# Hybrid decoder trunk: projection in groups of four row blocks, gates computed inside the last group, head norms and denominators with tokens on partitions, weights queued two tiles on

## The chip, the cores and the metric

The kernel runs on one core of one Trainium2 chip, in one launch. The metric is the device time of the program in microseconds. Before the change the median of three runs is 2245.18 us (2243.61 to 2250.87).

## The reference, cut to what matters

Two decoder layers over 256 tokens of width 2048, all in float32. Layer 0 mixes tokens with an mLSTM matrix memory, layer 1 with a gated linear recurrence; each mixer and each MLP has a modulated norm ahead of it and a gated residual behind it. The modulations come from a condition vector `c` through four 2048 x 6144 matrices.

```python
for layer in range(DEPTH):
    h, gate = ada_modulate(x, c, ada_w[layer, 0], ada_b[layer, 0])
    y = mlstm_mixer(h, ...) if layer % 2 == 0 else rglru_mixer(h, ...)
    x = x + gate * y
    h, gate = ada_modulate(x, c, ada_w[layer, 1], ada_b[layer, 1])
    x = x + gate * sq_relu_mlp(h, mlp_w1[layer], mlp_w2[layer])
return rms_norm(x) * final_g

# mlstm_mixer: one projection, then two chunks of 128 tokens, 8 heads, one state
q, k, v, o, ig, fg = jnp.split(h @ w_in, [...], axis=-1)
li = ig + b_gate[0]
lf = jax.nn.log_sigmoid(fg + b_gate[1])
#   in a chunk: b = cumsum(lf); m_t = running max; p = exp(d - m_t) * (q k^T)
num = w_inter * (q C) + p v
den = w_inter * (q n) + sum(p)
hh = num / max(|den|, exp(-m_t))
hh = hh * rsqrt(mean(hh * hh) + EPS)             # head norm, over the 256 values of a head
return (hh * norm_g * sigmoid(o)) @ w_out
```

## The kernel before

Activations lie transposed, features on partitions and the 256 tokens along the row; `xT[j]` is row block j of 16. A float32 matrix is multiplied in parts that TensorE takes at full pace: `split` (L167) cuts a weight tile of 128 x 2048, in two halves, into a rounded part `whi`, written by ScalarE (L174), and the rest `wlo`, written by VectorE (L175); `pair` (L179) does so for activations. Two halves of two tiles fit (`SPLIT_BUFS = 4`), so a tile is split when TensorE has done with the tile two before it. `mm3` (L192) makes three products of 256 columns for a block of 128 x 128 weights, `mm2` (L198) the same as one of 512 and one of 256.

Weight tiles come by `load` (L159) on the SyncE queue into a pool `raw` of four buffers. The modulations are done a 128 x 2050 tile at a time (`ada_tile`, L120): one DMA of 1025 KB and one VectorE instruction (L127). There are 192 such conditioning tiles. `fill` (L143) hands them out between weight tiles at a pace, and `need` (L149) when a modulation must be there. They land in `raw` too or, during the projection, in two buffers of their own (`adax`).

A scheduler orders each engine's instructions by program position; `tc.high_priority` moves the splits (200 positions) and the conditioning tiles (50) ahead. Each engine then works through its own row in order, so an instruction that waits holds up all behind it on its engine.

The stages that the change touches:

- **Projection of layer 0** (`group`, L487; products at L511). `GROUPS = (2, 4, 4, 4, 2)` row blocks of `h` are multiplied with 5120 columns of q, k, v and a part of o. A group of four has ten weight tiles, a group of two five. Each tile has 12288 columns to stream in products of 256 (q, k, o) or 512 (v). Between groups the partial sums rest in SBUF: ScalarE brings them back into PSUM (L526) and takes them out again (L537), 20 tiles of 128 x 512 a group. The first weight tile is used in float32, unsplit (`DIRECT`), and four products that compute nothing (`idle`, L540) follow group 0.
- **Gates** (L563 to L626). Ahead of the last group one more block (`gblk`) makes the 16 gate rows. Their log-sigmoid, cumulative sum and running maximum are a chain of small VectorE instructions on 8 x 256 (L583 to L613). `rows` goes to DRAM (L615) and comes back broadcast to all partitions: `mlast` (L617), and `MB` for each head (L634). The last group of two stands behind this in the program.
- **Heads** (`scores`, `state`, `head`, `meansq`, `normed`, L631 to L734). For each of eight heads: scores `sp`, transposed keys `kp`, state `cp`, numerator `num` with features on partitions. The denominator `den` (L675 to L677) and the mean square `hss` (L693, L694) are each computed with a matrix of ones as weights, so that every partition holds the same 256 sums, and `em`, `rs`, `rsu` work on 128 x 256 or 128 x 512 of them. Eight blocks of the rest of o (`ogate`, L703) lie in between where the table `OB` puts them.
- **Out projection** (L754 to L768). The first four output blocks are made together from four tiles `awoa` (the quads), the other twelve a tile `awo` each; `residual` (L332) adds each to `xT[j]`, and for the first eight makes `unnormed` for the MLP. All accumulate in five PSUM buffers (`MM_BUFS`).

Of the kernel before, what the change touches and what calls it, by code (L numbers as in the profile page):

```python
# [60 lines left out]
def trunk_kernel(ctx, tc, xT_d, par_d, ada_d, wqkv_d, wg_d, wo_d, awoa_d, awo_d, bwi_d, bg_d, bwo_d,  # L61
# [245 lines left out]
    def modulated(i, j, r, direct=False):  # L307
# [5 lines left out]
        if not direct:  # L313
            return pair(t, bias=mod[i][:, j:j + 1])
        h = act.tile([P, 2, S], F32, name="hdirect", tag="act")[:, 0, :]
        A.activation(h, t, AF.Identity, bias=mod[i][:, j:j + 1])
        return h, pair(h)
# [149 lines left out]
    def group_h(gi):  # L467
        h32 = []
        for kk in range(GROUPS[gi]):
            k = sum(GROUPS[:gi]) + kk  # L470
            if gi == 0:
                h, p = modulated(0, k, r, True)
                h32.append([h])
            else:
                p = modulated(0, k, r)
            hs.append(p)
        return h32

    raws = []

    def tile_ahead(nt, last):

        while len(raws) <= min(nt + AHEAD, last):
            raws.append(load(wqkv_d[len(raws)]))
        return raws[nt]

    def group(gi, h32):  # L487
# [4 lines left out]
        nt = per * k0 // 4  # L492
        width = DM // gn
        for nb in range(per * gn // 4):
            direct = nt in DIRECT
            gh = h32 if direct else [[p[:, 0, :], p[:, 1, :]] for p in hs[k0:k0 + gn]]
            w = tile_ahead(nt, per * (KC if gi == len(GROUPS) - 1 else KC - GROUPS[-1]) // 4 - 1)
            if not direct:
                w = split(w)
            nt += 1  # L500
# [39 lines left out]
    def idle(n, src):  # L540

        t = aux.tile([P, S], F32, name="idle", tag="aux")
        for _ in range(n):
            PE.matmul(t, lhsT=ones, rhs=src, start=True, stop=True)

    with ExitStack() as actx:
        adas.append(actx.enter_context(tc.tile_pool(name="adax", bufs=ADA_BUFS)))
        for gi in range(len(GROUPS) - 1):
            group(gi, group_h(gi))
            if gi == 0:  # L550
                idle(IDLE, ob[-1][:, 0, :])
        h32 = group_h(len(GROUPS) - 1)
        adas.clear()
# [4 lines left out]
    with ExitStack() as mctx:  # L558
        mp = mctx.enter_context(tc.tile_pool(name="mix0", bufs=1))
        scale = DQK ** -0.5  # L560


# [20 lines left out]
        def log1p(e, s, s2, q):  # L583

            V.tensor_scalar(out=s2, in0=e, scalar1=2.0, scalar2=None, op0=ALU.add)
            V.reciprocal(out=s, in_=s2)
            V.tensor_tensor(out=s, in0=s, in1=e, op=ALU.mult)
            V.tensor_tensor(out=s2, in0=s, in1=s, op=ALU.mult)
            V.tensor_scalar(out=q, in0=s2, scalar1=1.0 / 17, scalar2=None, op0=ALU.mult)
            for k in range(7, 0, -1):  # L590
                V.scalar_tensor_tensor(out=q, in0=q, scalar=1.0 / (2 * k + 1), in1=s2,
                                       op0=ALU.add, op1=ALU.mult)
            V.scalar_tensor_tensor(out=q, in0=q, scalar=1.0, in1=s, op0=ALU.add, op1=ALU.mult)
            return q

# [19 lines left out]
        nc.sync.dma_start(out=rows_d, in_=rows)  # L615
# [1 line left out]
        nc.sync.dma_start(out=mlast, in_=rows_d[:, 0, P - 1].partition_broadcast(P))  # L617
# [343 lines left out]
```

## Time and profile before

| | us |
|---|---|
| median of three runs | 2245.18 |
| the profiled execution | 2244.5 |
| its span, first to last instruction | 2242.8 |
| TensorE busy, weight loads busy | 2181.7, 1960.5 |
| VectorE, ScalarE, GpSimd busy | 1722.3, 1286.1, 90.1 |
| MLP of layer 0 and all behind it, from about 488.4 to the end | 1754.4 |

A row of the page or of a view names line, engine, operation and tiles (out<-in), a count, and a duration. "Idle before" is the time in which that engine had nothing to do ahead of the group, with the instruction that ended it. The windows view gives the busy time of each engine in a stretch, in brackets the number of its instructions, then TensorE's granted clock, the DMA engines' share and GB/s. A busy TensorE is not one at its peak, since products overlap: the number of products in a window tells its pace. A float32 product shows as two records, and some records of products are missing.

### The profile page before, as it was taken

How to read it: one execution, taken by the hardware profiler on the slowest of the kernel's cores; microseconds unless marked ns; L12 is line 12 of the kernel's file. 1: busy time of each engine (PE TensorE's matmuls, PEld its weight loads, DVE VectorE, ACT ScalarE, POOL GpSimd, SP SyncE). 2: the span in 40 equal slices, each digit the busy share in tenths (PEclk: the TensorE clock that was granted, in tenths of full speed). 3: DMA queues.
4: the chain of work that ended last, by engine and by line, in shares of the span. 5: the costliest groups of instructions: out<-in, count | busy, mean ns of one | idle time of the engine just before them, and what ended most of it. 6: DMA issues, size and time to landing. Idle time of an engine off the chain costs nothing.

```text
span 2242.8 us, 34191 instructions
## 1 busy us (share of the span) xinstructions
PE 2181.7 (97%) x13606; PEld 1960.5 (87%) x13606; DVE 1722.3 (77%) x2199; ACT 1286.1 (57%) x1997; POOL 90.1 (4%) x70
## 2 busy tenths in 40 slices
PE   7899899899999999999999999999999999999998
PEld 6798799788888889888889999889888889888887
DVE  6777888988898788888889988998875555555554
ACT  6677777345674335665445877756664334665443
POOL 0000010220000000000110000020000000000110
PEclk9999999899999999999999999999999999999999
DMA  8888887897788999998997665776875555555552
GB/s 345 348 325 319 307 300 255 303 337 270 285 284 319 337 322 332 328 334 319 322 335 276 211 229 208 269 276 238 307 284 203 188 188 188 188 188 188 189 188 93
DMA packets 88671, 601.25 MB, mean 268 GB/s; under 512 B 10424, under 2 KB 14648, under 8 KB 16192
## 3 DMA queue, kind: packets, MB, share of 16 engines
q1 hardware_dynamic: 86400, 598.03, 74.3%
q8 instruction: 106, 1.74, 0.3%
q10 hardware_dynamic: 2112, 1.05, 0.2%
q14 instruction: 53, 0.43, 0.1%
HBM read 596.93 MB, written 2.11 MB: 267 GB/s over the span
## 4 chain that ended last, share of the span: by engine, by line
PE 86%; DVE 7%; ACT 3%; issue 2%; DMA 1%; SPq 0%; DVEq 0%; ACTq 0%
PE mm L200 42%; PE mm L201 22%; PE mm L511 8%; DVE wlo L175 3%; PE mm L196 2%; PE mm L195 2%; PE mm L194 2%; DVE adaraw L127 2%; ACT whi L174 1%; PE mm L218 1%; PE mm L217 1%; PE mm L219 1%; DMA adaraw<-in_ada 1%; PE mm L357 0%; DVE hmod L311 0%
## 5 line engine op out<-in xcount | busy, mean ns | idle before, releaser
L200 PE MATMUL mm<-pair,whi 128*128 128x512 f32 x4272 | 1496.3, 394 | 5.0 <-DVE pair L188 3.2
L201 PE MATMUL mm<-pair,wlo 128*128 128x256 f32 x4272 | 1195.9, 280 | 0.8 <-DVE wlo L175 0.8
L175 DVE TENSOR_TENSOR wlo<-raw,whi 128x1024 fp32r<-128x1024 f32 x736 | 900.2, 1233 | 380.1 <-ACT whi L174 375.9
L174 ACT ACTIVATE whi<-raw 128x1024 fp32r<-128x1024 f32 x736 | 771.9, 1057 | 609.7 <-PE mm L200 476.7
L200 PEld LDWEIGHTS mm<-pair,whi 128*128 128x128 f32 x4272 | 802.6, 188 | 190.7 <-DVE pair L188 4.7
L201 PEld LDWEIGHTS mm<-pair,wlo 128*128 128x128 f32 x4272 | 804.7, 188 | 1.7 <-DVE wlo L175 1.1
L127 DVE SCALAR_TENSOR_TENSOR adaraw<-adaraw,cbc 128x2050 f32<-128x2050 f32 x192 | 439.7, 2291 | 50.7 <-DMA adaraw<-in_ada 41.7
L511 PE MATMUL mm<-pair,whi 128*128 128x256 f32 x736 | 136.0, 288 | 10.7 <-ACT pair L187 5.7
L511 PEld LDWEIGHTS mm<-pair,whi 128*128 128x128 f32 x736 | 115.8, 194 | 12.9 <-ACT pair L187 6.3
L194 PE MATMUL mm<-pair,whi 128*128 128x256 f32 x432 | 123.1, 285 | 0.0
L195 PE MATMUL mm<-pair,whi 128*128 128x256 f32 x432 | 122.0, 282 | 0.0
L196 PE MATMUL mm<-pair,wlo 128*128 128x256 f32 x432 | 121.4, 281 | 0.0
L511 PE MATMUL mm<-pair,wlo 128*128 128x256 f32 x368 | 104.0, 288 | 2.9 <-DVE wlo L175 2.9
L336 DVE SCALAR_TENSOR_TENSOR xall<-mm,mod,xall 128x256 f32<-128x256 f32 x170 | 81.0, 480 | 27.0 <-PE mm L201 18.7
L378 ACT ACTIVATE hsum<-hsum 128x256 f32<-128x256 f32 x121 | 49.2, 413 | 81.7 <-DVE hsum L261 71.3
L291 POOL TENSOR_TENSOR nacc<-nacc,nsq 128x256 f32<-128x256 f32 x52 | 75.6, 1453 | 351.0 <-ACT nsq L282 350.7
L196 PE MATMUL mm<-zhi,wlo 128*128 128x256 f32 x256 | 75.8, 296 | 6.6 <-DVE wlo L175 6.6
L194 PEld LDWEIGHTS mm<-pair,whi 128*128 128x128 f32 x432 | 81.9, 190 | 0.4
L194 PE MATMUL mm<-zhi,whi 128*128 128x256 f32 x256 | 74.9, 297 | 7.6 <-ACT zhi L731 5.5
L195 PEld LDWEIGHTS mm<-pair,whi 128*128 128x128 f32 x432 | 81.8, 189 | 0.0
L196 PEld LDWEIGHTS mm<-pair,wlo 128*128 128x128 f32 x432 | 81.8, 189 | 0.0
L511 PE MATMUL mm<-whi,pair 128*128 128x512 f32 x256 | 81.0, 394 | 0.0
(218 smaller groups left out, 2054.7 us busy)
## 6 DMA issues: line engine op xcount, KB each, us to landing
raw<-in_w SPq DMA_DIRECT2D x220, 1024.0 KB, 5.1
adaraw<-in_ada SPq DMA_DIRECT2D x192, 1025.0 KB, 6.6
raw<-in_wqkv SPq DMA_DIRECT2D x40, 1024.0 KB, 8.5
raw<-in_w1a SPq DMA_DIRECT2D x32, 1024.0 KB, 6.2
raw<-in_bwi SPq DMA_DIRECT2D x28, 1024.0 KB, 5.0
raw<-in_bwo SPq DMA_DIRECT2D x16, 1024.0 KB, 5.1
raw<-in_awo SPq DMA_DIRECT2D x12, 1024.0 KB, 5.5
raw<-in_wo SPq DMA_DIRECT2D x8, 1024.0 KB, 6.2
```

The source lines that it names most:

```text
L127: V.scalar_tensor_tensor(out=raw, in0=raw, scalar=1.0, in1=cbc, op0=ALU.mult, op1=ALU.mult, accum_out=mod[i][:, j:j + 1])
L174: A.activation(hi, sl, AF.Copy)
L175: V.tensor_tensor(out=lo, in0=sl, in1=hi.bitcast(F32), op=ALU.subtract)
L194: PE.matmul(out, lhsT=whi, rhs=hi, start=first, stop=False)
L195: PE.matmul(out, lhsT=whi, rhs=lo, start=False, stop=False)
L196: PE.matmul(out, lhsT=wlo, rhs=hi, start=False, stop=last)
L200: PE.matmul(out, lhsT=whi, rhs=p.rearrange("p a t -> p (a t)"), start=first, stop=False)
L201: PE.matmul(out[:, 0:S], lhsT=wlo, rhs=p[:, 0, :], start=False, stop=last)
L291: G.tensor_tensor(out=self.acc, in0=self.acc, in1=sq, op=ALU.add)
L336: V.scalar_tensor_tensor(out=xT[j], in0=acc[:, a:a + S], scalar=mod[i][:, 32 + j:33 + j], in1=xT[j], op0=ALU.mult, op1=ALU.add)
L378: A.activation(h, h, AF.Relu, bias=c)
L511: PE.matmul(out, lhsT=l, rhs=m, start=clear and kk + n == 0, stop=kk == gn - 1 and n == len(ops) - 1, skip_group_check=True)
```

## The change

- `GROUPS` is (4, 4, 4, 4): eight conditioning tiles now come ahead of the first product. The unsplit first tile and `idle` are gone.
- The gates are a function that is called inside the last group, ahead of its seventh tile (`GATES_AT = 6`); four tiles of the group stand behind it. The table `OB` now starts with 0 and has its eighth block at the last head.
- `den` and the sums of squares are products with one column: the data (`pT`, `qw`, `sq`) are the weights, a column of ones the moving operand. A pair of heads shares a tile `st` of 128 x 8 in PSUM, in one of the five buffers of the accumulators. `em` is made once for all heads, from a transpose of `rows`. The norm is then computed on 128 x 4, and four float32 products with the identity (`br`) spread it over the partitions again.
- All weight tiles from the projection to the first half of the MLP's first layer stand in a list `plan`; `weights` keeps two tiles beyond the present one queued.

```diff
-GROUPS = (2, 4, 4, 4, 2)
-DIRECT = (0,)
+GROUPS = (4, 4, 4, 4)
+GATES_AT = 6
-OB = (1, 1, 0, 1, 0, 1, 0, 1, 0, 1, 0, 1, 0, 1, 0, 0, 0)
+OB = (0, 1, 0, 1, 0, 1, 0, 1, 0, 1, 0, 1, 0, 1, 0, 1, 0)
-QKV_RATE = (1.6, 0.9, 0.9, 0.9, 1)
+QKV_RATE = (0.9, 0.9, 0.9, 0.9)
...
-        if adas and len(done) > 4 or len(done) % 2 < len(adas):
+        if adas and (len(done) > 8 or len(done) % 2 == 0):
...
     def weights(src):
-        return split(load(src))
+        if not plan:
+            return split(load(src))
+        while len(raws) < min(AHEAD + 1, len(plan)):
+            raws.append(load(plan[len(raws)]))
+        plan.pop(0)
+        return split(raws.pop(0))
...
         for nb in range(per * gn // 4):
+            if nb == GATES_AT and between is not None:
+                between()
+            w = weights(wqkv_d[per * k0 // 4 + nb])
...
+    last = 30 + GATES_AT
+    plan += [wqkv_d[n] for n in range(last)] + [wg_d] + [wqkv_d[n] for n in range(last, 40)]
+    plan += [wo_d[j] for j in range(16 - OG)] + [awoa_d[kg] for kg in range(4)]
+    plan += [awo_d[j] for j in range(4, KC)] + [w1a_d[0, j] for j in range(16)]
...
         nc.sync.dma_start(out=rows_d, in_=rows)
-        nc.sync.dma_start(out=mlast, in_=rows_d[:, 0, P - 1].partition_broadcast(P))
+        for c in range(2):
+            nc.sync.dma_start(out=mlast[:, c, :], in_=rows_d[:, c, P - 1].partition_broadcast(P))
+        for c in range(2):
+            gp = aux.tile([P, 2, H], F32, name="gp", tag="aux")
+            PE.transpose(out=gp[:, 0, :], in_=g[:, c * P:(c + 1) * P], identity=ident[0:H, 0:H])
+            PE.transpose(out=gp[:, 1, :], in_=rows[:, 1, c * P:(c + 1) * P], identity=ident[0:H, 0:H])
+            V.tensor_copy(out=gT[:, c, :], in_=gp[:, 0, :])
+            A.activation(em[:, c, :], gp[:, 1, :], AF.Exp, scale=-1.0)
...
+    group(len(GROUPS) - 1, gates)
...
-            PE.matmul(den[:, 0:P], lhsT=ones, rhs=pT[:, 0, :], start=True, stop=True)
-            PE.matmul(den[:, P:S], lhsT=ones, rhs=pT[:, 1, :], start=True, stop=False)
-            PE.matmul(den[:, P:S], lhsT=Cn[:, DV:DV + P], rhs=qw, start=False, stop=True)
-            A.activation(ad, den, AF.Abs)
-            V.scalar_tensor_tensor(out=em, in0=em, scalar=BIG, in1=ad, op0=ALU.min, op1=ALU.max)
-            A.activation(em, em, AF.Square, scale=EPS ** 0.5)
+            PE.matmul(st[:, 1, 0:1], lhsT=pT[:, 0, :], rhs=ones[:, 0:1], start=True, stop=True)
+            PE.matmul(st[:, 1, 1:2], lhsT=pT[:, 1, :], rhs=ones[:, 0:1], start=True, stop=False)
+            PE.matmul(st[:, 1, 1:2], lhsT=qw, rhs=Cn[:, DV:DV + 1], start=False, stop=True)
...
-            PE.matmul(ss, lhsT=ones, rhs=sq[:, 0, :], start=True, stop=False)
-            PE.matmul(ss, lhsT=ones, rhs=sq[:, 1, :], start=False, stop=True)
-            V.scalar_tensor_tensor(out=out, in0=ss, scalar=1.0 / DV, in1=em, op0=ALU.mult, op1=ALU.add)
+            for c in range(2):
+                for eb in range(2):
+                    PE.matmul(st[:, 0, c:c + 1], lhsT=sq[:, eb, c * P:(c + 1) * P], rhs=ones[:, 0:1],
+                              start=eb == 0, stop=eb == 1)
...
-        def normed(h2, rs):
-            rsqrt(rs, rs, 1.0, TINY)
+        def normed(h2, st):
+            A.activation(d, st[:, :, 1, :], AF.Abs)
+            V.scalar_tensor_tensor(out=d, in0=ec, scalar=BIG, in1=d, op0=ALU.min, op1=ALU.max)
+            V.scalar_tensor_tensor(out=d, in0=d, scalar=EPS, in1=d, op0=ALU.mult, op1=ALU.mult)
+            V.scalar_tensor_tensor(out=x, in0=st[:, :, 0, :], scalar=1.0 / DV, in1=d, op0=ALU.mult,
+                                   op1=ALU.add)
+            rsqrt(rs, x, 1.0, TINY)
+            for i in range(2):
+                for c in range(2):
+                    PE.matmul(br[:, i, c * P:(c + 1) * P], lhsT=rs[:, i, c:c + 1].broadcast_to([P, P]),
+                              rhs=ident, start=True, stop=True)
```

How the scheduler's rows change is shown at three places. TensorE, before, first at the scores of head 0 (behind the last group and one o block; L194 to L196 are products of the next o block), then at the numerator of head 0, which 42 more products of that block stand ahead of:

```order
L639 MATMUL sp<-qk_187,qk_191 128x128 x2
L641 MATMUL kp<-ident,qk_191 128x128
L194 MATMUL mm<-pair,whi 128x256
L195 MATMUL mm<-pair,whi 128x256
L196 MATMUL mm<-pair,wlo 128x256
```

```order
L195 MATMUL mm<-pair,whi 128x256
L196 MATMUL mm<-pair,wlo 128x256
L671 MATMUL num<-E,v_195 128x128
L672 MATMUL num<-E,v_196 128x128
L673 MATMUL num<-qw,Cn 128x128
```

TensorE, after, at the same place; its first row is the end of the first o block, which follows the last group:

```order
L204 MATMUL mm<-pair,wlo 128x256
L596 MATMUL gp<-ident,g 128x8 x2
L621 MATMUL sp<-qk_187,qk_191 128x128 x2
L597 MATMUL gp<-ident,rows 128x8
L623 MATMUL kp<-ident,qk_191 128x128
L597 MATMUL gp<-ident,rows 128x8
L641 MATMUL cp<-v_195,kw 128x256
L642 MATMUL cp<-ones,kw 128x1
L652 MATMUL num<-E,v_195 128x128
L653 MATMUL num<-E,v_196 128x128
L654 MATMUL num<-qw,Cn 128x128
```

The o block that stood between the scores and the numerator now stands behind the numerator. In rows behind the block of gates TensorE had five weight tiles and two o blocks up to the numerator, and has four tiles and one o block now.

VectorE, before, at the end of the gate chain (`ls2`, `lf`, `g`, `rows` are the chain; `wlo` belongs to the tile `raw` named beside it, here of the last group; `adaraw` are conditioning tiles):

```order
L591 SCALAR_TENSOR_TENSOR ls2_2346<-ls2_2346 8x256
L127 SCALAR_TENSOR_TENSOR adaraw_2583,mod0_127<-adaraw_2583,cbc_98 128x2050
L593 SCALAR_TENSOR_TENSOR ls2_2346<-ls2_2346,lse_2343 8x256
L127 SCALAR_TENSOR_TENSOR adaraw_2630,mod0_127<-adaraw_2630,cbc_98 128x2050
L599 SCALAR_TENSOR_TENSOR lf_2361<-ls2_2346,li_2340 8x256
L175 TENSOR_TENSOR wlo_2634<-raw_2537,whi_2633 128x1024
L607 SCALAR_TENSOR_TENSOR lf_2361<-ones_85,lf_2361 8x128
L175 TENSOR_TENSOR wlo_2638<-raw_2537,whi_2637 128x1024
L609 TENSOR_TENSOR g_2363<-li_2340,lf_2361 8x128
```

VectorE, after, at the same place (`raw_2614` and `raw_2715` are the second and third o block):

```order
L183 TENSOR_TENSOR wlo_2824<-raw_2614,whi_2823 128x1024
L545 SCALAR_TENSOR_TENSOR ls2_2419<-ls2_2419 8x256
L183 TENSOR_TENSOR wlo_2828<-raw_2614,whi_2827 128x1024
L547 SCALAR_TENSOR_TENSOR ls2_2419<-ls2_2419,lse_2416 8x256
L126 SCALAR_TENSOR_TENSOR adaraw_2678,mod0_127<-adaraw_2678,cbc_98 128x2050
L575 SCALAR_TENSOR_TENSOR lf_2434<-ls2_2419,li_2413 8x256
L612 TENSOR_SCALAR halfg_2685<-par_78 128x16
L583 SCALAR_TENSOR_TENSOR lf_2434<-ones_85,lf_2434 8x128 x2
L585 TENSOR_TENSOR g_2436<-li_2413,lf_2434 8x128 x2
L587 SCALAR_TENSOR_TENSOR rows_2437<-g_2436 8x128
L183 TENSOR_TENSOR wlo_2958<-raw_2715,whi_2957 128x1024
L589 TENSOR_TENSOR rows_2437<-lf_2434,rows_2437 8x128
```

From the gate block's evacuation to the last row of the chain there were four tiles to split and four conditioning tiles; now there are six and four, and the sixth is that of the third o block.

VectorE, before, at the last two heads (`rs`, `em`, `rsu` on 128 x 256 and 128 x 512; all `adaraw` are conditioning tiles):

```order
L695 SCALAR_TENSOR_TENSOR rs_3516<-hss_3655,em_3623 128x256
L175 TENSOR_TENSOR wlo_3969<-raw_3966,whi_3968 128x1024
L175 TENSOR_TENSOR wlo_3973<-raw_3966,whi_3972 128x1024
L271 SCALAR_TENSOR_TENSOR rsu_3660<-rs_3516,rsy_3659 128x512
L127 SCALAR_TENSOR_TENSOR adaraw_4028,mod1_128<-adaraw_4028,cbc_98 128x2050
L272 SCALAR_TENSOR_TENSOR rsu_3660<-rsu_3660,rsy_3659 128x512
L127 SCALAR_TENSOR_TENSOR adaraw_4036,mod1_128<-adaraw_4036,cbc_98 128x2050
L273 SCALAR_TENSOR_TENSOR rs_3516<-rsu_3660,rsy_3659 128x512
```

VectorE, after, at the end of the quads, behind that norm (`mm_3651` and the two behind it are accumulators of the quads, `raw_3771` and `raw_3829` the first two `awo` tiles):

```order
L126 SCALAR_TENSOR_TENSOR adaraw_3908,mod1_128<-adaraw_3908,cbc_98 128x2050
L183 TENSOR_TENSOR wlo_4016<-raw_3829,whi_4015 128x1024
L126 SCALAR_TENSOR_TENSOR adaraw_3920,mod1_128<-adaraw_3920,cbc_98 128x2050
L183 TENSOR_TENSOR wlo_4020<-raw_3829,whi_4019 128x1024
L126 SCALAR_TENSOR_TENSOR adaraw_3927,mod1_128<-adaraw_3927,cbc_98 128x2050
L126 SCALAR_TENSOR_TENSOR adaraw_3935,mod1_128<-adaraw_3935,cbc_98 128x2050
L340 SCALAR_TENSOR_TENSOR xall_80<-mm_3651,mod0_127,xall_80 128x256
L340 SCALAR_TENSOR_TENSOR xall_80<-mm_3652,mod0_127,xall_80 128x256
```

In the changed kernel no conditioning tile stands between the last head's numerator and its norm any more; five stand behind it and ahead of the first residual.

More of the change, by code (lines that the diff above doesn't have):

```diff
@@ L312, in modulated @@
                                op0=ALU.mult, op1=ALU.mult)
[L313 to L317, printed above, removed]
+        return pair(t, bias=mod[i][:, j:j + 1])
     def unnormed(i, j):
@@ L465, in trunk_kernel, with group @@
     ob = [act.tile([P, 2, S], F32, name="th", tag="act") for s in range(OG // 2)]
[L467 to L487, printed above, removed]
+    def group(gi, between=None):
         gn, k0 = GROUPS[gi], sum(GROUPS[:gi])
         per = (4096 + OG * P) // 512
-        nt = per * k0 // 4
         width = DM // gn
+        hs.extend(modulated(0, k0 + kk, r) for kk in range(gn))
+        gh = [[p[:, 0, :], p[:, 1, :]] for p in hs[k0:]]
         for nb in range(per * gn // 4):
[L495 to L500, printed above, removed]
+            if nb == GATES_AT and between is not None:
+                between()
+            w = weights(wqkv_d[per * k0 // 4 + nb])
             def part(kk, o, n):
-                if direct:
-                    return [w[:, kk * width + o:kk * width + o + n]]
                 o += kk % (gn // 2) * width
@@ L538, in group @@
             fill(1, QKV_RATE[gi])
[L540 to L553, printed above, removed]
+    last = 30 + GATES_AT
+    plan += [wqkv_d[n] for n in range(last)] + [wg_d] + [wqkv_d[n] for n in range(last, 40)]
+    plan += [wo_d[j] for j in range(16 - OG)] + [awoa_d[kg] for kg in range(4)]
+    plan += [awo_d[j] for j in range(4, KC)] + [w1a_d[0, j] for j in range(16)]
+    actx = ExitStack()
+    adas.append(actx.enter_context(tc.tile_pool(name="adax", bufs=ADA_BUFS)))
+    for gi in range(len(GROUPS) - 1):
+        group(gi)
     qT = [qk[h // 2][:, h % 2, :] for h in range(H)]
@@ L556, in trunk_kernel, with log1p, gates @@
     vh = [[vs[h // 2 * 2 + t][:, h % 2, :] for t in range(2)] for h in range(H)]
-    with ExitStack() as mctx:
-        mp = mctx.enter_context(tc.tile_pool(name="mix0", bufs=1))
-        scale = DQK ** -0.5
+    rows_d = dram.tile([H, 2, S], F32, name="rows_d")
+    mlast = const.tile([P, 2, H], F32, name="mlast")
+    gT = const.tile([P, 2, H], F32, name="gT")
+    em = const.tile([P, 2, H], F32, name="em")
+    wk = const.tile([P, H], F32, name="wk")
+    def log1p(e, s, s2, q):
+        V.tensor_scalar(out=s2, in0=e, scalar1=2.0, scalar2=None, op0=ALU.add)
+        V.reciprocal(out=s, in_=s2)
+        V.tensor_tensor(out=s, in0=s, in1=e, op=ALU.mult)
+        V.tensor_tensor(out=s2, in0=s, in1=s, op=ALU.mult)
+        V.tensor_scalar(out=q, in0=s2, scalar1=1.0 / 17, scalar2=None, op0=ALU.mult)
+        for k in range(7, 0, -1):
+            V.scalar_tensor_tensor(out=q, in0=q, scalar=1.0 / (2 * k + 1), in1=s2,
+                                   op0=ALU.add, op1=ALU.mult)
+        V.scalar_tensor_tensor(out=q, in0=q, scalar=1.0, in1=s, op0=ALU.add, op1=ALU.mult)
+        return q
+    def gates():
         gblk = block([wg_d], hs)
@@ L581, in trunk_kernel @@
         A.activation(e, e, AF.Exp, scale=-1.0)
[L583 to L594, printed above, removed]
         at = log1p(e, row("ls"), row("ls2"), row("lq"))
@@ L631, in scores @@
         def scores(h):
-            MB = mp.tile([P, 2, S], F32, name="MB", bufs=MB_BUFS)
-            nc.sync.dma_start(out=MB.rearrange("p r t -> p (r t)"),
-                              in_=rows_d[h].rearrange("r t -> (r t)").partition_broadcast(P))
+            MB = mp.tile([P, S], F32, name="MB", bufs=MB_BUFS)
+            nc.sync.dma_start(out=MB, in_=rows_d[h, 0].partition_broadcast(P))
             sp = aux.tile([P, 2, P], F32, name="sp", tag="aux")
@@ L740, in trunk_kernel @@
             if h % 2 == 0:
-                rs = act.tile([P, 2, S], F32, name="rs", tag="act")
-            kw, E, qw, em = sc
+                st = ps.tile([P, 2, 2, 2], F32, name="st", tag="mm")
+            kw, E, qw = sc
             Cn = state(h, kw)
             ogate(OB[1 + 2 * h])
-            hbh, sq, em = head(h, E, qw, em, Cn)
+            hbh, sq = head(h, E, qw, Cn, st[:, h % 2])
             hbs.append(hbh)
```

56 lines of the change are left out of this document (26 added, 30 removed).

## The prediction

> **What bounds the kernel now.** I read the page first, then the windows, the chain, and the timelines around the gates and the heads.
>
> ```profile
> PE 2181.7 (97%) x13606; PEld 1960.5 (87%) x13606; DVE 1722.3 (77%) x2199; ACT 1286.1 (57%) x1997; POOL 90.1 (4%) x70
> ```
>
> TensorE is busy for all but 61 us. What an edit can win is work that it no longer does, and those gaps. The windows show where they lie (time, TensorE, weight loads, VectorE, ScalarE, GpSimd, clock, DMA):
>
> ```profile
> 60.00:70.00 10.00, 3.78 (x26) 3.02 (x24) 8.36 (x10) 2.91 (x4) 0.00 (x0) 0.96 0.93 361
> 70.00:80.00 10.00, 9.96 (x61) 9.95 (x62) 3.95 (x4) 5.42 (x8) 0.00 (x0) 0.69 0.98 412
> 80.00:90.00 10.00, 10.00 (x88) 10.00 (x87) 9.92 (x11) 8.68 (x14) 0.00 (x0) 1.00 0.77 290
> 182.00:244.30 62.30, 58.65 (x385) 52.16 (x384) 47.63 (x44) 40.32 (x60) 0.00 (x0) 1.00 0.82 310
> 260.00:270.00 10.00, 5.85 (x38) 5.85 (x38) 9.84 (x12) 8.55 (x14) 0.00 (x0) 0.83 0.78 275
> 390.00:400.00 10.00, 4.40 (x35) 4.07 (x34) 10.00 (x13) 3.98 (x4) 0.00 (x0) 1.00 0.99 357
> 400.00:410.00 10.00, 6.91 (x30) 6.61 (x31) 7.36 (x10) 2.33 (x4) 0.00 (x0) 0.52 0.92 327
> 430.00:440.00 10.00, 5.94 (x33) 5.74 (x32) 10.00 (x12) 4.29 (x7) 3.87 (x2) 0.73 0.87 307
> 650.00:700.00 50.00, 50.00 (x288) 43.74 (x287) 46.45 (x65) 30.09 (x51) 0.00 (x0) 1.00 0.86 311
> ```
>
> Full pace is 88 products of 256 columns in 10 us, 0.1136 us each. So a projection tile (12288 columns) or an o block (48 such products) is worth 5.45 us. The gate block is 16 pairs of `mm2`; the last row has 288 such products in 50 us, so a pair is 0.347 us and the block 5.6. Behind 510 us I find no gap that the change touches. In 390 to 400 and 430 to 440 VectorE is full while TensorE starves. After each pause the clock falls: 70 to 80 holds 61 products, 3 us short. I charge 3 us for a long pause.
>
> **The start.** The chain:
>
> ```profile
> 5.03 14.80 DMA adaraw<-in_ada
> 19.85 2.30 DVE adaraw L127 x2
> 24.59 31.48 PE mm L511 x176
> 70.03 109.93 PE mm L511 x714
> ```
>
> Now eight conditioning tiles come ahead of the first product, not four. The row of 19.85 is the fourth. Four more are 4.2 MB, 10 us at the 412 GB/s above, so the eighth lands at 29.6 instead of 19.8. Then follow its VectorE instruction (2.3), the pairs and the first split (0.5, 1.05, 1.2): products flow at 36, with half of a cold start still charged at 38.5. Five tiles at 5.45 end at 65.8. Before, five tiles ended and the sixth began at 70.0, cold, in effect 73. **-7.2.** The pause at 56 to 70, when group 1 waited for conditioning, goes: eight are handed out over ten tiles.
>
> A boundary between groups falls at the tenth tile, with an evacuation (0.6), a pair (0.5) and a split (1.06 and 1.23) one behind the other, estimated at +3. At the end of the stage ScalarE's row puts a split behind the evacuation of the tile's first half; that cost some 0.8 us a tile in ten tiles (182 to 244, 62.3 us against 54.5), and will in nine: -1. That group's window stands among the rows above. The gate block took 244.3 to 253.7 for 5.6 us of products; inside a group I charge it 2 us of loss, not 3.8: -1.8. Together **-7.0**. The 40 evacuations and reloads saved (0.6 us each) are on ScalarE beside full TensorE and count nothing but this. The gate block ends at 252 (T below), with one tile more behind it than before, where T was 253.7.
>
> **The gates.** What follows T before, from four timelines:
>
> ```profile
> 253.76 0.38 ACT L260 ACTIVATE gacc<-mm 128x256 f32<-128x256 f32 x1 [2.78 <-PE mm L201]
> 262.25 0.41 ACT L581 ACTIVATE lse<-lse 8x256 f32<-8x256 f32 x1
> 284.63 0.28 DVE L613 TENSOR_TENSOR rows<-lf,rows 8x128 f32<-8x128 f32 x1
> 284.93 0.35 SPq L615 DMA_DIRECT2D rows_d<-rows  x1
> 286.42 1.22 SPq L617 DMA_DIRECT2D mlast<-rows_d  x1
> 287.68 1.10 SPq L634 DMA_DIRECT2D MB<-rows_d  x2
> 295.09 0.70 ACT L646 ACTIVATE E<-MB,gT 128x128 f32<-128x128 f32 x2 [0.54 <-DMA MB<-rows_d]
> 305.33 0.38 PE L671 MATMUL num<-E,v 128*128 128x128 f32 x2
> ```
>
> The chain takes 31.2 us to `rows`, 10.2 more through DRAM to the first exponential, 3 to the numerator: 44. TensorE had 5 tiles and 2 blocks, 38.2 us, to cover it, and reached the numerator at T+51.6, 13.4 lost, most of it elsewhere (260 to 270). Now it has 4 tiles and 1 block, 27.3. The durations:
>
> ```profile
> L175 DVE TENSOR_TENSOR wlo<-raw,whi 128x1024 fp32r<-128x1024 f32 x736 | 900.2, 1233 | 380.1 <-ACT whi L174 375.9
> L174 ACT ACTIVATE whi<-raw 128x1024 fp32r<-128x1024 f32 x736 | 771.9, 1057 | 609.7 <-PE mm L200 476.7
> L127 DVE SCALAR_TENSOR_TENSOR adaraw<-adaraw,cbc 128x2050 f32<-128x2050 f32 x192 | 439.7, 2291 | 50.7 <-DMA adaraw<-in_ada 41.7
> L591 DVE SCALAR_TENSOR_TENSOR ls<-ls 8x256 f32<-8x256 f32 x7 | 2.9, 411 | 0.2
> L586 DVE RECIPROCAL lse<-ls 8x256 f32<-8x256 f32 x1 | 1.7, 1741 | 0.0
> ```
>
> On VectorE stand ahead of `rows`: six tiles to split (14.8), four conditioning tiles (9.2 and 0.3 of read-out) and 10.6 of chain, 35 us. (The same count for before, with four tiles, gives 30 against the 31.2 seen.) It also waits: `lse` is on ScalarE behind two evacuations and two splits, ready at T+12 and not T+8.9, and each split waits for TensorE, the last, of the third o block, for the end of the first at T+29. I get `rows` at T+41. On SyncE a conditioning tile and two `mlast` (1.22 each) stand ahead of `MB`: the exponential at T+52, the numerator at T+55.5, 3 more for the cold clock. TensorE stands from T+30 with nothing else in its row. Lost 58.5 - 27.3 = 31.2 instead of 13.4: **+17.8.** I bound it by 8 (nothing but what TensorE lacks: two of 5.45, less 3) and 26 (each of four conditioning tiles 2 us late).
>
> **The heads.** Rows of a float32 product of 128 columns, of the mean square, and VectorE's in 290 to 410:
>
> ```profile
> 305.55 0.39 PE L672 MATMUL num<-E,v 128*128 128x128 f32 x2
> 305.77 0.39 PE L673 MATMUL num<-qw,Cn 128*128 128x128 f32 x2
> ...
> 361.00 0.68 PE L693 MATMUL hss<-hsq,ones 128*128 128x256 f32 x2
> 361.52 0.59 PE L694 MATMUL hss<-hsq,ones 128*128 128x256 f32 x2
> ```
> ```profile
> L681 DVE SCALAR_TENSOR_TENSOR em<-em,ad 128x256 f32<-128x256 f32 x8 | 3.4, 420 | 0.3 <-ACT ad L680 0.3
> L695 DVE SCALAR_TENSOR_TENSOR rs<-hss,em 128x256 f32<-128x256 f32 x8 | 3.3, 418 | 0.6 <-PE hss L694 0.6
> L271 DVE SCALAR_TENSOR_TENSOR rsu<-rs,rsy 128x512 f32<-128x512 f32 x4 | 2.8, 694 | 2.0 <-ACT rsy L270 1.9
> ```
>
> A head had four products of 0.22 (`den`, `cp` by ones) and 0.9 of `hss`: 1.8 us. Now it has eight of one column. No row shows one; it lies between nothing and the 0.23 of two passes that each keep the 0.1136 pace with their weight load. I take 0.15: 1.2 a head, 8 x 0.6 = 4.8 won, four `br` of 4 x 0.22 lost (3.5), and some 1 for `num`'s shorter partners: **-2.3**, between -10 and +4.
>
> The Trainium skill, TensorE: Matmul & The Clock Gate, section LDWEIGHTS, has a weight load cost by its columns, 128 / 1.2 = 107 ns. By that rule two passes with nothing to stream under are 0.21 us, as dear as the products replaced; the estimate would be 4 us more, 2248. No row here shows an uncovered load.
>
> VectorE is relieved of 8 x 0.84 and four times 2.1, less 24 tiny ones of some 0.15: 11 us. A head now asks 7.9 us of it and 9.2 of TensorE, where both asked 9.5.
>
> **Norm of the last heads and out projection.** The two stretches up to 488.4, and two rows of VectorE:
>
> ```profile
> 305.30:388.00 82.70, 82.70 (x659) 80.17 (x658) 71.18 (x97) 61.28 (x118) 7.79 (x6) 1.00 0.74 265
> 388.00:488.40 100.40, 84.86 (x643) 83.53 (x643) 91.56 (x103) 40.12 (x65) 25.53 (x14) 0.90 0.90 325
> ...
> 398.63 0.69 DVE L273 SCALAR_TENSOR_TENSOR rs<-rsu,rsy 128x512 f32<-128x512 f32 x1
> 411.68 1.66 DVE L336 SCALAR_TENSOR_TENSOR xall<-mm,mod,xall 128x256 f32<-128x256 f32 x4 [0.37 <-PE mm L196]
> ```
>
> From numerator 0 to the MLP before: 183.1 us for 6 blocks (32.7), heads (32) and 768 products (87.2), so 31 lost. 12.6 of it is 390 to 410: conditioning tiles between the pieces of the last norm. That goes: the new order has none there, and an o block and 106 products cover the chain. But the tiles only move. Five of them now stand ahead of the first residual, and the second `awo` block needs the accumulator that this residual frees. From the last `br`, TensorE ends the quads and one block at 22.9; VectorE, splitting and conditioning, comes to the residual at 27.9: 5.4 lost. Then two conditioning tiles a block (4.6), a split (2.4), residual and `unnormed` (1.1) ask 8 us of VectorE against 5.45: 2 to 3 lost in each of four blocks. With 2 for GpSimd's adds I get 17.4 lost there and 5 in the heads, 22.4 against 31: **-8.7**, between -16 and -2. Queueing two on costs nothing by itself: the buffers of `raw` are still four.
>
> **Sum** against the profiled execution, 2244.5, which is 0.7 under the median: -7.0 + 17.8 - 2.3 - 8.7 = -0.2, so 2244. The MLP would begin at 488.2 and runs as before.
>
> **Rivals.** No change is what I forecast, and 0.3% (6.7 us) is about what a measurement can tell. (1) Faster: VectorE, relieved, keeps up in the out projection, whose loss falls to 8, and `rows` comes at T+36 by the plain count of 35: 2244 - 9 - 5 = 2230. For it: its 95% busy rows end at the heads. Against: eight us a block. (2) Slower: the gate chain becomes the bound. Each us of `rows` behind T+41 is one of TensorE; from T+48 the kernel is slower by 6.7. Four conditioning tiles each landing 3 us late would do: 2244 + 12 = 2256. For it: SyncE waits mostly for these two buffers. Against: 41.7 us of 439 is all that VectorE ever waited for them, mostly at the start. (3) One-column products as dear as 0.23: 2248. (4) The start pays nothing, for group 0 waits on DMA: +7, 2251.
>
> **How the numbers follow.** Forecast 0.34, (1) 0.32, (2) 0.20, (3) 0.08, (4) 0.06. Same is the forecast with (3): 0.42; faster is (1): 0.32; slower is (2) with (4): 0.26. The half widths of the terms' bounds, 5 for the start (rival 4 pays it nothing), 9, 7 and 7, add as independent ones to 14; the range goes a little past that and past (1) and (2) on both sides, 2227 to 2261.
>
> **What would show it.** First projection product near 34 to 36; no pause at 56 to 70; TensorE empty for some 20 us or more ahead of numerator 0, released by `E` or `Cn` and behind that `MB`; the last norm without a pause; a wait for the first residuals. Wrong if that first pause is under 10 us (then faster), or if the out projection still holds TensorE for 25 us.

## The result

The changed kernel takes 2270.95 us (median of 4 runs, 2266.32 to 2276.74), the kernel before 2245.6: a ratio of 1.011, 95% interval 1.008 to 1.0141. It is slower by some 25 us, where the forecast was no change (2244) and the range ended at 2261. The profiled execution is the slowest of the four, 2276.74 us with a span of 2275.0, so a comparison of the two traces holds about 6 us more than the medians do.

Four points of the program cut both traces into pieces: T, the evacuation of the gate block; numerator 0; the first product of the MLP of layer 0; the end. Each row is read from the timelines and the span of that kernel's trace.

| | first split product | T | numerator 0 | MLP begins | from there to the end |
|---|---|---|---|---|---|
| before | 33.2 | 253.8 | 305.3 | 488.1 | 1754.8 |
| after | 37.9 | 258.7 | 309.8 | 505.6 | 1769.4 |

Since one tile more lies ahead of T now and one o block more behind numerator 0 (5.45 us each), the pieces compare like this. Up to T: 5.0 - 5.45 = **-0.5**. From T to numerator 0, 51.1 us for 27.3 of work, so 23.8 lost and not 13.4, and 6.6 lost to a low clock behind it: **+17.0**. From there to the MLP 195.8 - 5.45 - 6.6 = 183.7 against 182.7: **+1.0**. From the MLP to the end **+14.6**. Together 32.1 of the spans' 32.2.

### The profile page after: what moved, and what is told of

The parts are those of the page before. It is cut to its first block, busy times and chain, and to the rows that moved or that the text cites. A ratio compares the mean times of both kernels' runs of the same rounds, so it can differ in the third digit from the quotient of the medians.

```text
span 2275.0 us, 34314 instructions
## 1 busy us (share of the span) xinstructions
PE 2191.3 (96%) x13680; PEld 1970.3 (87%) x13680; DVE 1712.6 (75%) x2197; ACT 1258.8 (55%) x1939; POOL 75.3 (3%) x70
## 4 chain that ended last, share of the span: by engine, by line
PE 84%; DVE 8%; ACT 3%; issue 2%; DMA 2%; SPq 0%; DVEq 0%; ACTq 0%
PE mm L208 42%; PE mm L209 21%; PE mm L491 9%; DVE wlo L183 3%; PE mm L204 2%; PE mm L202 2%; PE mm L203 2%; DVE adaraw L126 2%; ACT whi L182 1%; DMA adaraw<-in_ada 1%; PE mm L227 1%; PE mm L226 1%; PE mm L225 1%; DVE hmod L319 1%; DVE pair L196 0%
## 5 line engine op out<-in xcount | busy, mean ns | idle before, releaser
L491 PE MATMUL mm<-pair,whi 128*128 128x256 f32 x768 | 139.6, 285 | 24.9 <-ACT whi L182 22.4
L202 PE MATMUL mm<-pair,whi 128*128 128x256 f32 x432 | 123.4, 286 | 0.0
L203 PE MATMUL mm<-pair,whi 128*128 128x256 f32 x432 | 123.2, 285 | 0.0
L340 DVE SCALAR_TENSOR_TENSOR xall<-mm,mod,xall 128x256 f32<-128x256 f32 x170 | 81.1, 480 | 26.6 <-PE mm L209 19.0
L225 PE MATMUL mm<-unnormed,whi 128*128 128x258 f32 x272 | 77.6, 285 | 0.0
```

The source lines that it names most:

```text
L202: PE.matmul(out, lhsT=whi, rhs=hi, start=first, stop=False)
L203: PE.matmul(out, lhsT=whi, rhs=lo, start=False, stop=False)
L225: PE.matmul(out[:, 0:UX], lhsT=whi, rhs=u[:, 0:UX], start=first, stop=False)
L340: V.scalar_tensor_tensor(out=xT[j], in0=acc[:, a:a + S], scalar=mod[i][:, 32 + j:33 + j], in1=xT[j], op0=ALU.mult, op1=ALU.add)
L491: PE.matmul(out, lhsT=l, rhs=m, start=clear and kk + n == 0, stop=kk == gn - 1 and n == len(ops) - 1, skip_group_check=True)
```

## The profile after

The timelines of the changed kernel around the gates (start, duration, engine, line, instruction; in brackets the idle time ahead of it and what ended it):

```profile
258.73 0.39 ACT L268 ACTIVATE gacc<-mm 128x256 f32<-128x256 f32 x1 [1.57 <-PE mm L209]
287.77 0.28 PE L204 MATMUL mm<-pair,wlo 128*128 128x256 f32 x1
293.55 0.47 PE L596 MATMUL gp<-ident,g 8*128 8x8 f32 x2 [5.49 <-DVE g L585]
296.91 0.28 DVE L589 TENSOR_TENSOR rows<-lf,rows 8x128 f32<-8x128 f32 x1
299.81 3.55 SPq L617 DMA_DIRECT2D MB<-rows_d  x2
305.76 0.69 ACT L628 ACTIVATE E<-MB,gT 128x128 f32<-128x128 f32 x2 [6.07 <-DMA MB<-rows_d]
308.52 1.22 PE L641 MATMUL cp<-v,kw 128*128 128x256 f32 x2 [10.64 <-ACT kw L625]
309.82 0.78 PE L652 MATMUL num<-E,v 128*128 128x128 f32 x2
```

TensorE ends the first o block at 287.8, T+29, as forecast; `rows` is done at T+38.5 (forecast T+41), the exponential stands at T+47 (T+52), the numerator at T+51 (T+55.5). Between 287.8 and 309.8 TensorE has only the scores, transposes and the state of head 0. The windows show that pause, the clock behind it, and two stretches of the MLP (time, TensorE, weight loads, VectorE, ScalarE, GpSimd, clock, DMA share, GB/s):

```profile
290.00:300.00 10.00, 2.57 (x9) 1.82 (x9) 9.48 (x18) 0.36 (x2) 0.00 (x0) 0.50 0.24 86
300.00:310.00 10.00, 1.48 (x5) 1.30 (x6) 3.30 (x6) 2.33 (x9) 0.81 (x2) 0.50 0.87 238
310.00:320.00 10.00, 10.00 (x46) 9.82 (x47) 3.63 (x5) 3.14 (x9) 2.33 (x1) 0.50 0.76 236
320.00:330.00 10.00, 10.00 (x72) 10.00 (x71) 3.37 (x4) 4.52 (x9) 0.00 (x0) 0.79 0.29 98
...
505.60:530.60 25.00, 19.59 (x126) 17.85 (x125) 23.33 (x37) 11.66 (x19) 0.00 (x0) 0.86 0.83 292
605.60:630.60 25.00, 22.07 (x116) 18.70 (x115) 21.66 (x35) 13.47 (x27) 0.00 (x0) 0.93 0.70 261
```

From 310 to 330 there are 118 products where full pace has 176: 58 x 0.1136 = 6.6 us, at a clock of 0.50 to 0.79.

Behind 505 VectorE's own row shows what the MLP waited for:

```profile
505.23 2.36 DVE L183 TENSOR_TENSOR wlo<-raw,whi 128x1024 fp32r<-128x1024 f32 x2 [1.50 <-ACT whi L182]
507.50 2.29 DVE L126 SCALAR_TENSOR_TENSOR adaraw<-adaraw,cbc 128x2050 f32<-128x2050 f32 x1
509.72 0.48 DVE L340 SCALAR_TENSOR_TENSOR xall<-mm,mod,xall 128x256 f32<-128x256 f32 x1
511.69 2.36 DVE L183 TENSOR_TENSOR wlo<-raw,whi 128x1024 fp32r<-128x1024 f32 x2 [1.50 <-ACT whi L182]
513.97 2.29 DVE L126 SCALAR_TENSOR_TENSOR adaraw<-adaraw,cbc 128x2050 f32<-128x2050 f32 x1
516.18 0.42 DVE L279 SCALAR_TENSOR_TENSOR rsu<-ss,rsy 128x256 f32<-128x256 f32 x1
523.96 0.79 PE L208 MATMUL mm<-pair,whi 128*128 128x512 f32 x1 [5.42 <-DVE pair L196]
```

The last residual of the out projection (L340) stands behind a weight tile's split and a conditioning tile, and the norm (L279) behind another of each: it comes 10.6 us after the MLP's first product. TensorE then waits 5.4 us for the first pairs. The two stretches of 25 us in the windows hold 126 and 116 products.

## The experiments

Fifteen kernels ran. Times are medians, ratios against the kernel before on the same chip. The changed kernel's own interval, 1.008 to 1.0141, is 7 us either way, so a gain of a few us against it is not shown by the medians alone.

**e1, the gates earlier.** `-GATES_AT = 6`, `+GATES_AT = 0`.

> The gates are called ahead of the first tile of the last group, not ahead of its seventh; nothing else is changed. In the changed kernel TensorE stood from 287.8 to 309.5 between the first o block and numerator 0, and its clock was 0.50 to 0.79 from 310 to 330, some 6 us more. Theory A (the gate chain lacks cover): ten tiles and a block, 60 us, now cover a chain of about 50, the pause goes and with it the cold clock: 18 to 28 us less, 2243 to 2253. Rival B (VectorE's total of splits, conditioning tiles and chain is the limit, wherever the chain stands): the pause comes back as waits inside the last group, gain under 8 us, 2263 or more.

2259.24 us, ratio 1.0066 (1.0051 to 1.0081): 11.7 won, between the two theories. The gate chain was done at 260.5, long before the o block ended, and yet numerator 0 stood at 296.3, behind two waits of 2.6 and 4.9 us. Two rows of SyncE's timeline in this kernel, and one of its waits from 278 to 292:

```profile
260.50 0.35 SPq L590 DMA_DIRECT2D rows_d<-rows  x1
289.61 0.80 SPq L617 DMA_DIRECT2D MB<-rows_d  x2
```
```profile
SPq L617 <- DVE halfg L612: 5.4, 1, 5.4
```

The broadcasts `MB` waited for `halfg`, the first tile of the heads' own pool, which VectorE wrote right behind the last conditioning tile from `adax`. So the heads could not begin before the group's conditioning tiles were through. That the pool takes the place of `adax` in memory is argued from the code, not tried. Theory A holds for the chain and falls for the pause.

**e2, two o blocks ahead of numerator 0.** Only the table `OB` is that of before.

> Only the table of the o blocks is that of before: two blocks ahead of numerator 0, none at the last head. Theory A: one block more covers the gate chain, the pause ahead of numerator 0 falls by 5.5, and the last norm loses its block, which costs up to 5: 2265 to 2271. Rival B: the block's split on VectorE pushes the chain back as far as it covers, no gain at numerator 0, and the last norm's loss stands alone: 2271 to 2277.

2267.56, ratio 1.0103 (1.0088 to 1.0118): 3.4 won, as by A, but within the changed kernel's interval. Numerator 0 stands at T+50.9 with one block more in the cover.

**e3, no list behind the projection.**

```diff
-    plan += [wo_d[j] for j in range(16 - OG)] + [awoa_d[kg] for kg in range(4)]
-    plan += [awo_d[j] for j in range(4, KC)] + [w1a_d[0, j] for j in range(16)]
```

> The list of weights queued two ahead holds only the projection and the gate block; the o blocks, the out projection and the MLP load a tile where it is split. From the MLP's first product to the end the changed kernel took some 9 to 15 us longer than before, and the out projection waited 3 us at each of four blocks for the split. Theory C (tiles queued two ahead hold the raw buffers that conditioning tiles need, and shift these in VectorE's row to where TensorE waits): 8 to 15 us less, 2256 to 2263, the gates' pause unchanged. Rival D (these waits come from the number of conditioning tiles due there, not from the queue): 2268 to 2274.

2255.06, ratio 1.0045 (1.0028 to 1.0062): 15.9 won, as by C or a little more. Numerator 0 to MLP takes 186.7 us, not 195.8, and MLP to end 1757.0, not 1769.4. The gates' pause is as it was (T+51.5).

**e4, the old groups.** `GROUPS = (2, 4, 4, 4, 2)`, their rates, gates ahead of the last group.

> Groups of 2, 4, 4, 4, 2 with before's rates of conditioning tiles, gates ahead of the last group of two; the unsplit first tile and the idle products stay out, all else as in the changed kernel. Theory E (groups of four pay nothing at the start; the later first product costs what the pause at 56 to 70 cost): the gate block ends within 3 us of where it would by the changed kernel less one tile, 253.3. Five tiles and one block cover the chain, one tile more than in the changed kernel: 2262 to 2269. Rival F (groups of four won the 7 us of the forecast and lost them elsewhere): the gate block ends at 258 or later.

2259.49, ratio 1.0069 (1.0054 to 1.0084). The gate block ends at 250.9, 2.4 us earlier than theory E's 253.3: groups of four pay nothing. (In the ten kernels whose program is that of the changed kernel up to there, T lies between 256.3 and 258.7, so 2.4 is no more than scatter.) Numerator 0 at T+48.3.

**e5 and e6**, e1 and e4 each without the list.

> Gates ahead of the last group (as in e1) and the list ending with the projection (as in e3). Theory: the cover of the gate chain and the queue of weights are two separate costs, 11.7 and 15.9 us, and add up: 2243. Rival: both draw on one thing, VectorE's and the queue's backlog around the heads, so that either edit alone already wins most of it: 2250 to 2255. In e1 the broadcasts MB stood in SyncE's queue from 263 to 289.6 behind tiles queued ahead; if that was all that was left of the pause there, this kernel comes below the sum, 2236 to 2240.

> Groups of before (as in e4), gates ahead of the last group of two, and the list ending with the projection. By the sum of e4 (-11.5) and e3 (-15.9): 2243 to 2245. If groups of four pay for themselves once their gate chain is covered, e5 is faster than this by 5 or more; if they pay nothing, the two agree within 3.

2250.94, ratio 1.0024 (1.0010 to 1.0037), and 2251.66, ratio 1.0033 (1.0021 to 1.0045). They agree within 1 us: the groups pay nothing. Both are 8 us above the sums. That would mean that most of what an earlier gate chain wins and half of what the list costs is paid in one place; but each sum carries the 7 us of the changed kernel, so this is not shown.

**e7, the old head norms**, on e3: `den` and `hss` by a matrix of ones, `em` and `rs` on wide tiles, no `st`.

> As e3 (2255), with denominators and mean squares as before: products with a matrix of ones as weights, sums on all partitions, the norm on 128 x 512. From the traces a head takes about 0.9 us less in the changed kernel, and no norm arithmetic on wide tiles is left on VectorE: if that is so this kernel is 5 to 8 us slower than e3, 2260 to 2263. By my forecast's term, 2.3 us: 2257. Rival (the price of one-column products is that of the products replaced): 2254 to 2256.

2240.63, ratio 0.9977 (0.9967 to 0.9987): not 5 to 8 slower than e3 but 14.4 faster. Every reading of mine on the heads missed. The rows of TensorE showed why: between the transposes of the gates and numerator 0 the scheduler had put 86 products of o blocks, where it puts none in e3 and in the changed kernel. Numerator 0 itself came no earlier, T+49.6. What differed for these products was `st`, which lies among the five accumulators (tag `mm`). That is tried in e9 and e10.

**e8, one tile ahead** behind the projection, not two.

> The list stays, but behind the projection only one tile beyond the present one is queued, not two. Theory C (a tile that waits in one of four raw buffers keeps a conditioning tile out, and these then come late and together): one buffer less is held, half or more of the 16 us comes back, 2256 to 2264. Rival (the order in SyncE's queue alone, whatever is held): 2268 to 2273.

2272.0, ratio 1.0125 (1.0110 to 1.0141). Nothing comes back, so theory C falls: holding one tile instead of two costs the same. No kernel has a list that holds no buffer.

**e9 and e10, `st` moved**, in the changed kernel and in e3.

```diff
-                st = ps.tile([P, 2, 2, 2], F32, name="st", tag="mm")
+                st = aux.tile([P, 2, 2, 2], F32, name="st", tag="aux")
```

> The changed kernel with one edit: st, the tile of a pair's sums, is taken from the three buffers of scores, states and numerators and not from the five of the accumulators. In the built order 96 products of o blocks then stand between the transposes of the gates and numerator 0, where the changed kernel has none. Theory G (st's place among the accumulators keeps the next o block behind numerator 0, and the pause there and the cold clock behind it are the loss): 96 products are 10.9 us that move into a pause of 20, and the clock stays up: 12 to 17 us less, 2254 to 2259. Rival H (the new head norms are slow in themselves: short products, their waits): 2268 to 2272.

> The same edit on e3 (2255). Theory G: as e7, whose old head norms used no accumulator: 2238 to 2243. If the new head norms win the 2.3 us of the forecast by themselves, 1 to 3 below e7's 2240.6. Rival H: 2252 to 2256.

2256.41, ratio 1.0045 (1.0031 to 1.0059), and 2241.92, ratio 0.9981 (0.9971 to 0.9991): 14.5 and 13.1 us won by moving one tile, as by theory G. The windows of e9 at the place of the pause:

```profile
290.00:300.00 10.00, 9.79 (x78) 9.11 (x77) 9.94 (x20) 2.64 (x5) 0.00 (x0) 1.00 0.28 85
300.00:310.00 10.00, 8.47 (x72) 8.22 (x71) 3.92 (x7) 2.88 (x10) 0.82 (x2) 1.00 0.92 244
310.00:320.00 10.00, 9.86 (x80) 9.27 (x80) 6.34 (x9) 8.48 (x20) 1.81 (x2) 1.00 0.88 309
320.00:330.00 10.00, 10.00 (x87) 9.95 (x86) 9.58 (x16) 6.02 (x8) 0.91 (x1) 1.00 0.94 349
```

TensorE holds 150 products in the 20 us where it held 14, and the clock stays at 1.00. Numerator 0 stands at T+50.3 as ever. e10 is faster than both kernels, and e7 agrees with it: with that mended, the new head norms and the old cost the same. Two tenths of a per cent is all that these kernels win on the kernel before.

**e11 and e12**, on e10: the gates ahead of the fifth tile (`GATES_AT = 4`); the rows' way through DRAM on GpSimd's queue.

> As e10, with the gates ahead of the fifth tile of the last group (six tiles behind them, not four). If the gate chain still leaves a pause in e10, two tiles more, 10.9 us, cover it; the order has 48 products there instead of 90, so the net cover is 6 us more: 2233 to 2239. If the pause is gone already or is SyncE's and not VectorE's, no change: within 3 of e10.

> As e10, with the rows' way through DRAM (to rows_d, mlast, MB) on GpSimd's queue, not SyncE's, where it stood behind tiles that waited for buffers. If that wait is part of the pause ahead of numerator 0: 2 to 6 us below e10. If VectorE's rows come too late anyway: within 2 of e10.

2254.94, ratio 1.0043 (1.0029 to 1.0057), and 2249.89, ratio 1.0016 (1.0007 to 1.0025). Both missed, on the slow side. In e12 the trip itself was longer: `rows_d` left at 296.65, `mlast` only at 301.15, and the numerator stood at T+55.4, 5 later. In e11 the numerator stood at T+51.5 and its clock fell to 0.50 behind it; but 196.1 us from there to the MLP, against e10's 173.4, is 15 more than I can account for by products. That stays open.

**e13 and e14, the list without the MLP's tiles**, in the changed kernel and in e9. `- + [w1a_d[0, j] for j in range(16)]`.

> The changed kernel with the list ending at the out projection: only the 16 tiles of the MLP's first half of the first layer leave it. With st mended, the kernel with the list (e9) and the one without (e10) differ by 14.4 us, and the traces put nearly all of it behind the MLP's first product: 1772 us from there to the end with the list, 1758 without, with 22 and 37 products fewer in two stretches of 25 us. Theory J (the list costs through the MLP's tiles: split as soon as they are there, ahead of the norm's own chain on VectorE): 9 to 14 us less, 2257 to 2262. Rival K (it costs in the heads and the out projection, where e3 won 9 of its 16): 2265 to 2271.

> Both edits on the changed kernel: st among the buffers of scores and numerators (e9, 2256.4), and the list without the MLP's tiles. Theory J: 2242 to 2246, as e10. Rival K: 2250 to 2256.

2261.79, ratio 1.0083 (1.0070 to 1.0096): 9.2 won, in the range of J. 2252.87, ratio 1.0036 (1.0024 to 1.0048): 3.5 won, in the range of K. Both intervals meet those of the kernels they are compared with, so the medians do not decide between J and K. In the traces the MLP's part is alike, 1759.1 us to the end (10.3 less) and 1761.0 (11.2 less). But that overstates the gain, since the cut itself moves. TensorE's row in e13, from the last product of the out projection to the first of the MLP:

```profile
497.15 0.28 PE L204 MATMUL mm<-zhi,wlo 128*128 128x256 f32 x1
498.25 0.70 PE L309 MATMUL ss<-nacc,ones 128*128 128x256 f32 x2 [0.81 <-POOL nacc L299]
...
500.95 0.39 PE L225 MATMUL mm<-unnormed,whi 128*128 128x258 f32 x1 [1.57 <-ACT whi L182]
```

TensorE now waits ahead of the MLP's first product, which starts 3.8 us behind the last one of the out projection, in e14 too; in the changed kernel, e9 and e10 it is 0.1. Counted from that last product to the end, e13 and e14 win 6.7 and 7.6 us, not 10.3 and 11.2. And from numerator 0 up to it e14 takes 175.4, e9 175.9 and e10 173.3. The windows of e13, to compare with the two stretches above:

```profile
500.90:525.90 25.00, 22.85 (x147) 21.58 (x148) 23.46 (x40) 14.79 (x24) 0.00 (x0) 0.86 0.77 282
...
600.90:625.90 25.00, 25.00 (x144) 21.89 (x143) 24.11 (x39) 17.93 (x34) 0.00 (x0) 1.00 0.75 274
```

147 and 144 products, where the changed kernel had 126 and 116. In e13 the norm's first step on VectorE stands at 500.28, 3.1 us behind the last product of the out projection, where the changed kernel has it 10.7 behind.

**e15, the list alone, on the kernel before**, of its `awo` and MLP tiles.

> The kernel before, with a list of its awo tiles and the MLP's 16 tiles queued two ahead from the out projection on, and nothing else of the change. Theory J: the same waits appear behind the MLP's first product, 8 to 14 us more than before, 2253 to 2260. If the list only costs together with the other parts of the change (the order that they leave VectorE in): within 4 of before, 2242 to 2250.

2245.51, ratio 1.0009 (1.0000 to 1.0018): no change that matters, so theory J's total fails. The MLP does lose: 1768.5 us from the last product of the out projection, 13.7 more than before. But heads and out projection win most of it back: from numerator 0 to that product they take 172.0, not 182.6. And the norm is hardly late here, 6.9 us behind that product against 5.6 before. TensorE waits for the pairs behind it:

```profile
502.96 0.50 PE L207 MATMUL mm<-pair,whi 128*128 128x512 f32 x1 [2.27 <-DVE pair L195]
```

Seen over all traces: the seven kernels whose list holds the MLP's tiles take 1765.8 to 1772.2 us from the MLP to the end, the others, the kernel before among them, 1754.8 to 1761.7, except e11 with 1766.0, whose profiled execution is 6.2 above its median. With the waits ahead of the MLP added, e13 and e14 have 1762.9 and 1764.8, and the two sets all but meet.

## Why the prediction was wrong

The MLP of the first layer was said to begin at 488.2 and to run "as before"; it began at 505.6 and ran 14.6 us longer.

**Queueing two on.** "Queueing two on costs nothing by itself: the buffers of `raw` are still four" is the step that failed. Taken out, the list gives back 15.9 us (e3), and 14.5 with `st` mended (e9 to e10). I had priced what the list holds; one tile held or two is the same (e8). What it changes is the order. In the changed kernel the last residual stands behind a split and a conditioning tile, 4.1 us after the MLP's first product, and the norm at 10.6. In the kernel before, whose MLP begins at 488.1, the residual comes first, and the norm at 5.4:

```profile
488.25 0.48 DVE L336 SCALAR_TENSOR_TENSOR xall<-mm,mod,xall 128x256 f32<-128x256 f32 x1 [0.17 <-PE mm L196]
488.65 2.35 DVE L175 TENSOR_TENSOR wlo<-raw,whi 128x1024 fp32r<-128x1024 f32 x2
490.92 2.29 DVE L127 SCALAR_TENSOR_TENSOR adaraw<-adaraw,cbc 128x2050 f32<-128x2050 f32 x1
...
493.49 0.42 DVE L271 SCALAR_TENSOR_TENSOR rsu<-ss,rsy 128x256 f32<-128x256 f32 x1 [0.28 <-ACT rsy L270]
```

The late norm is only a part of the loss. The second stretch, 100 us on, lacks 28 products against e13, some 4.9 us (a pair of them is 0.347 in the prediction). There the list ends, and TensorE waits for a split behind a conditioning tile whose data land late:

```profile
605.56 2.29 DVE L126 SCALAR_TENSOR_TENSOR adaraw<-adaraw,cbc 128x2050 f32<-128x2050 f32 x1 [1.26 <-DMA adaraw<-in_ada]
607.78 2.35 DVE L183 TENSOR_TENSOR wlo<-raw,whi 128x1024 fp32r<-128x1024 f32 x2
609.05 0.38 PE L209 MATMUL mm<-pair,wlo 128*128 128x256 f32 x1 [2.25 <-DVE wlo L183]
```

In the traces the MLP's tiles in the list cost 6.7, 7.6 and 13.7 us behind the out projection's last product, in three pairs (e13, e14, e15). Ahead of it the list's sign varies: 9.0 lost in the changed kernel, 2.6 in e9, 10.6 won on the kernel before. Why its order there helps or harms is not settled. Nor is the list dear everywhere: one of the `awo` and MLP tiles alone, on the kernel before, costs nothing in total (e15). The order of the out projection was shown in the text on the change; that of the MLP's start I did not read, since I had found no gap behind 510.

**The gates.** +17.8 was forecast and +17.0 came. All the pieces were earlier than said, by 2.5 for `rows` and 4.4 for the numerator, and the clock behind the pause cost 6.6, not 3. The reason beneath was only half seen. I took it that TensorE "stands from T+30 with nothing else in its row" because the change had moved the o block. But an o block could have stood there: with `st` off the accumulators the scheduler puts 96 products between the gates' transposes and numerator 0 (139 more in all behind T, by the trace), which wins 14.5 us. In all kernels with four to six tiles behind the gates numerator 0 came at T+48 to T+55; what is lost is what TensorE lacks in that time. How `st` keeps the block back in the scheduler is not shown, only that it does.

**The heads.** One-column products were taken at 0.15 us. The timeline of TensorE in the changed kernel, at full clock:

```profile
344.99 0.95 PE L670 MATMUL st<-ones,hsq 128*128 128x1 f32 x8
345.80 0.36 PE L202 MATMUL mm<-pair,whi 128*128 128x256 f32 x1
...
348.28 0.28 PE L655 MATMUL st<-ones,E 128*128 128x1 f32 x2
348.43 0.36 PE L656 MATMUL st<-ones,E 128*128 128x1 f32 x2
348.65 0.36 PE L657 MATMUL st<-Cn,qw 128*128 128x1 f32 x2
348.87 0.69 PE L621 MATMUL sp<-qk,qk 128*128 128x128 f32 x4
```

Four take 0.81 and delay the next product by 0.08: 0.22 each. Three take 0.59: 0.20 each. So they cost what the products of 128 columns cost that they replace, as rival (3) had it, and with `br` the term is some +2, not -2.3. The rule cited from the Trainium skill, TensorE: Matmul & The Clock Gate, section LDWEIGHTS, two weight loads of 107 ns, 0.21 us, agrees with this row.

**The start.** -7.0 was forecast, -0.5 came, in size as rival (4) had it. Its reason, that group 0 waits on DMA, is not seen: behind its first product TensorE waits 2.4 us in all up to 120, for pairs. That product flowed at 37.9, not 36: on VectorE conditioning tiles of 2.29 us stand between the pieces of the first pairs. The rest went to the groups: from 40, the start with its cold clock, to T are 218.7 us for 36 tiles and the gate block (201.8), so 17 lost, where I counted 12. e5 and e6 agree within 1 us: the pause that groups of two had at 56 to 70 is worth no more than the later start. Leaving out the unsplit first tile and the idle products was not tried alone.

**The out projection.** -8.7 with the last norm was forecast; heads and out projection together came to +1.0, not -11.0. The last norm's pause did go (TensorE is full from 330 to 420). The wait for the first residuals came (2.6 us, up to 423.3, where 5.4 was forecast). But then TensorE waited for a split at one block after the other:

```profile
442.05 0.42 ACT L290 ACTIVATE nsq<-xall 128x256 f32<-128x256 f32 x1 [0.66 <-DVE xall L340]
442.75 0.28 PE L204 MATMUL mm<-zhi,wlo 128*128 128x256 f32 x1
444.98 1.99 ACT L182 ACTIVATE whi<-raw 128x1024 fp32r<-128x1024 f32 x2
446.07 0.39 PE L202 MATMUL mm<-zhi,whi 128*128 128x256 f32 x1 [3.04 <-ACT whi L182]
...
466.51 0.48 DVE L340 SCALAR_TENSOR_TENSOR xall<-mm,mod,xall 128x256 f32<-128x256 f32 x1 [2.53 <-PE mm L204]
468.44 0.39 PE L202 MATMUL mm<-zhi,whi 128*128 128x256 f32 x1 [1.97 <-ACT whi L182]
```

ScalarE's row has the split of the next tile behind the square (`nsq`) of a residual. Such waits of 2.0 to 3.0 us end at 446.1, 456.8 and 468.4, and the clock is 0.85, 0.84 and 0.79 in the three stretches of 10 us from 440 on. At the first the residual stood behind a conditioning tile on VectorE. At the other two it waited for the last product of its block, so that TensorE stood through residual, square and split.

**The rivals.** (3), and (4) in its size, 0.14 of the chance together, came true. (1) failed at both of its places. (2) named the gate chain as the bound, with `rows` too late; `rows` came early. None of them held the list.

## What to carry to other kernels

Where a chain's length hardly moves, as T to numerator 0 here, count what the busy engine has to do in the meantime, and then ask what keeps other ready work out of the gap: a small tile taken from the accumulators' pool cost 13 to 14.5 us here. An earlier load need not be free even where it holds nothing that is needed: it makes later work ready sooner, and in the changed kernel that work stood ahead of steps that TensorE waited for. Read the rows of the built order to the end of the stages that any moved transfer feeds, and past the place where the list ends, not only where the old profile had gaps. And where two kernels are cut at an instruction, look whether a wait has moved across the cut.
